# Down projection with 22 of 44 pairs by seven block products, their weight sums made by DRAM-to-DRAM adding transfers

## The chip, the core and the metric

The kernel runs on one core of a Trainium2 chip. The core has a matrix engine (TensorE, PE in the profile, with its weight loads shown apart as PEld), a vector engine (VectorE, DVE), a scalar engine (ScalarE, ACT), a general engine (GpSimd, POOL) and a sync engine that here only issues transfers (SyncE, SP). Each engine works through its own list of instructions in order and waits for the others by semaphores. Sixteen DMA engines move data between the memory off the core (DRAM) and the core's SBUF; they take their work from queues that SP, ACT and POOL feed. The matrix engine adds its products up in a third memory, PSUM.

The metric is the time of one execution on the device in microseconds (us); for several runs the median. The profile comes from one more execution and counts from its first to its last instruction (the span).

## The reference

One encoder block on 256 tokens of 2048 features, in float32. The change touches only the down projection at the end of the gated channel mixer:

```
def conv_glu(hn, w_up, conv_w, conv_b, w_down):
    up = hn @ w_up                                  # 256x2048 @ 2048x11264
    gate, val = jnp.split(up, 2, axis=-1)           # two halves of 5632
    gate = dwconv_centred(gate, conv_w, conv_b)     # three taps along the tokens
    return (jax.nn.gelu(gate, approximate=True) * val) @ w_down   # 256x5632 @ 5632x2048
...
    ff = conv_glu(hn, w_ffn_up[i], ffn_conv_w[i], ffn_conv_b[i], w_ffn_down[i])
    h = h + rmsnorm(ff, ffn_norm_post[i])
```

## The kernel before, in words

**Products in three parts.** float32 values are split into a high part, rounded to the matrix engine's short float32 form, and a low part, the rest. A product of two float32 matrices is then three products: high by high, high by low, low by high. `split` (line 138) does it for weights: a copy on ACT writes the high part (line 147), a subtraction on DVE writes the low part (line 148). Its results rotate through five buffers of 1056 columns for the high and five for the low parts. `raw` (line 151) loads 1 MB of weights over SP's queue into one of three buffers.

**The stages.** In order of time: input projection and the sequence mixers, output projection (`wo`), up projection, down projection (`dn`), gate of the last mixer (`gt`). The up projection runs in 11 slabs of 512 hidden features (loop at line 796). For each slab `feature_pairs` (line 293) is called twice for the gate half (`ga`, weights `ug`) and twice for the value half (`va`, weights `uv`); each call loads two pieces of 1 MB and does 128 products of the matrix engine. So a slab loads eight pieces. Between the two halves comes the convolution on ACT and DVE (line 805), the Gelu on ACT (line 806), and on POOL a multiplication by the tokens' norm factors (line 807). DVE then takes the value sums out of PSUM and multiplies them by POOL's result (line 815) into `hid`, which holds all 5632 hidden features.

**The down projection** (`sublayer("dn", ...)`, line 859) takes the 2048 output columns in two halves. Each half walks over the 5632 hidden features in 22 pairs of 128-feature blocks (`token_major`, line 246); a pair loads 1 MB of `w_down` (two blocks of 128 rows, 1024 columns). A plain pair takes 24 products of 128x512 (two blocks, two token halves, two column halves, three parts).

**Seven block products.** For pairs named in `fast`, `seven_products` (line 201) writes the 2x2 by 2x2 block product with seven products in place of eight, which is Strassen's and Winograd's scheme: 7 times 3 products, 21 in place of 24. It needs sums of weight blocks, which DVE makes in place in the load buffer (lines 209 to 211), and sums of blocks of the hidden values, which `pair_sums` makes (line 709, lines 712 to 715 and the split in lines 716 and 717). It splits 3584 columns of weights (512 + 3 x 1024) where a plain pair splits 2048. Before, pairs 2, 5, 8, 11, 14, 17 of the first half and 2, 5, 8, 11, 14, 17, 19 of the second go this way, 13 in all. `hid_sums` (line 840) keeps the sums of four pairs in two pages for the second half. At the end of each half `combine` (line 222) adds the shared products up in PSUM.

**Buffers.** Pages of 2048 columns rotate through 13 buffers (`page`, line 70). During the up projection the four pages of its input `hf` are among them; they come free at its end. Nothing in the kernel before is issued on POOL's DMA queue.

Of the kernel before, what the change touches and what calls it, by code (L numbers as in the profile page):

```python
# [51 lines left out]
def build(nc, a, out):  # L52
# [5 lines left out]
    with tile.TileContext(nc) as tc, \  # L58
            tc.tile_pool(name="const", bufs=1) as cp, \
            tc.tile_pool(name="weights", bufs=1) as wp, \  # L60
            tc.tile_pool(name="pages", bufs=1) as gp, \
            tc.tile_pool(name="small", bufs=1) as sp, \
            ExitStack() as early, \
            tc.tile_pool(name="pmain", bufs=6, space=bass.MemoryType.PSUM) as pm, \
            tc.tile_pool(name="pmisc", bufs=2, space=bass.MemoryType.PSUM) as pc:

        def ins(r):
            return getattr(r, "ins", r)
# [41 lines left out]
        vt = cp.tile([P, V_N - V_SCW], F32, name="vt")  # L110
        small = ep.tile([P, 80 + 512], F32, name="small")

        last = {}

        def load(dst, src, ahead=False):

            with tc.issue_after(last["dma"]) if last and not ahead else nullcontext():
                return ins(nc.sync.dma_start(dst, src))
# [31 lines left out]

        def raw(name, src, a_, b_):
            r = wp.tile([P, 2048], F32, tag="raw", bufs=3, name=name)
            last["dma"] = load(r[:, :a_ * b_].rearrange("p (a b) -> p a b", a=a_), src, True)
            return r

# [42 lines left out]
                yield o, c  # L198
                c += o.shape[-1]

        def seven_products(name, r, a_, acc, alt, start, stop):

            v = r.rearrange("p (b c) -> p b c", b=4)
            b11 = split(f"{name}a", r[:, :512], 512)
            b2 = split(f"{name}b", r[:, 1024:], 1024)

            nc.vector.tensor_sub(v[:, 0:2], v[:, 1::2], v[:, 0:2])
            nc.vector.tensor_sub(v[:, 3], v[:, 3], v[:, 0])  # L210
            nc.vector.tensor_sub(v[:, 2], v[:, 2], v[:, 3])
            t13 = split(f"{name}c", r[:, :1024], 1024)
            t42 = split(f"{name}d", r[:, 1024:], 1024)
            for x, (wh, wl), c, o, own in (
                    ("a11", b11, 0, alt[0], True), ("a12", b2, 0, acc[0][0], False), ("s4", b2, 512, acc[0][1], False),
                    ("s1", t13, 0, alt[1], True), ("s3", t13, 512, alt[2], True), ("a22", t42, 0, acc[1][0], False),
                    ("s2", t42, 512, alt[3], True)):
                xh, xl = a_[x]
                for q, (xx, ww) in enumerate(((xh, wh), (xh, wl), (xl, wh))):
                    mm(o, xx, ww[:, c:c + 512], own and start and q == 0, own and stop and q == 2)  # L220

        def combine(name, acc, alt, cut):


            m = [mid(f"{name}v{i}") for i in range(2)]
            p1, s16, s165, s167 = (m[i // 2][:, i % 2 * 512:(i % 2 + 1) * 512] for i in range(4))

            def add(o, a_, b):
                nc.vector.tensor_add(o, a_, b)

            nc.scalar.copy(p1, alt[0])
            add(s16, alt[3], p1)
            add(acc[0][0], acc[0][0], p1)
            add(s165, alt[1], s16)
            add(acc[0][1], acc[0][1], s165)
            add(s167, alt[2], s16)
            add(acc[1][0], acc[1][0], s167)
            add(s165, alt[2], s165)
            if cut:
                o = acc[1][1]  # L240
                acc[1][1:] = [o[:, :256], alt[0][:, :256]]
                add(acc[1][2], o[:, 256:], s165[:, 256:])
                s165 = s165[:, :256]
            add(acc[1][1], acc[1][1], s165)

        def token_major(name, w, c0, ks, get, acc, tail=1, fast=(), alt=None, sums=None):


            group, nu = [], len(ks) // 2
            for u in range(nu):  # L250
                k0 = ks[2 * u]
                r = raw(f"{name}r{k0}", w[k0 * P:(k0 + 2) * P, c0:c0 + 1024]
                        .rearrange("(k p) c -> p k c", p=P), 2, 1024)
                if u in fast:
                    if u == fast[0]:
                        alt = alt + [misc(f"{name}s{i}") for i in (2, 3)]
                    seven_products(f"{name}{k0}", r, sums(k0), acc, alt, u == fast[0], u == fast[-1])
                    continue
                for j in range(2):
                    group.append((k0 + j, *split(f"{name}{k0}_{j}", r[:, j * 1024:(j + 1) * 1024], 1024)))  # L260
                if nu - tail <= u < nu - 1:
                    continue

                order = [(t, o, g, q) for t in range(2) for o in columns(acc[t]) for g in group for q in range(3)] \
                    if u == nu - 1 or u - 1 in fast[-1:] else \
                    [(t, o, g, q) for g in group for t in range(2) for q in range(3) for o in columns(acc[t])]
                for t, (o, c), (k, wh, wl), q in order:
                    xh, xl = (v[:, t * P:(t + 1) * P] for v in get(k))
                    xx, ww = ((xh, wh), (xh, wl), (xl, wh))[q]
                    mm(o, xx, ww[:, c:c + o.shape[-1]], k == ks[0] and q == 0, k == ks[-1] and q == 2)  # L270
                if u - 1 in fast[-1:]:
                    combine(name, acc, alt, nu - tail == u + 1 and tail > 1)
                group = []
                aside()
# [434 lines left out]
        def pair_sums(name, s, o, a11, a21, a12, a22):  # L709

            s1, s2, s3, s4 = (s[:, i * P:(i + 1) * P] for i in range(4))
            nc.vector.tensor_add(s1, a21, a22)
            nc.vector.tensor_sub(s3, a11, a21)
            nc.vector.tensor_sub(s2, s1, a11)
            nc.vector.tensor_sub(s4, a12, s2)
            nc.scalar.copy(o[:, :512], s[:, :512])
            nc.vector.tensor_sub(o[:, 512:], s[:, :512], o[:, :512].bitcast(F32))
            return {f"s{i + 1}": (o[:, i * P:(i + 1) * P], o[:, 512 + i * P:512 + (i + 1) * P]) for i in range(4)}
# [70 lines left out]
                      V_FN, Pairs, ((5,), (2, 4)), Sums("cs", cat))  # L789


        pl = [ple(0)]
        rf = row_rstd("rf", h)
        rfb = along_tokens("rfb", rf)
        hid = [page(f"hid{i}") for i in range(6)]
        for s in range(DFF // 512):
            sc = mid(f"gr{s}")
            for i in range(2):
                ga = main(f"ga{s}{i}")
                feature_pairs(f"ug{s}{i}", w_up, s * 512 + i * 256, hf, ga)  # L800
                o = sc[:, i * 512:(i + 1) * 512]
                total(o, ga)
                v = o.rearrange("p (f t) -> p f t", f=2)
                nc.vector.tensor_tensor(v, v, rfb.unsqueeze(1).to_broadcast([P, 2, L]), op=ALU.mult)
            cv = conv(f"fc{s}", sc, 3, V_FCW + 4 * s, NF, V_FCB + 4 * s)
            nc.scalar.activation(cv, cv, AF.Gelu_apprx_tanh)  # L806
            nc.gpsimd.tensor_tensor(cv.rearrange("p (f t) -> p f t", f=4), cv.rearrange("p (f t) -> p f t", f=4),  # L807
                                    rfb.unsqueeze(1).to_broadcast([P, 4, L]), op=ALU.mult)
            for i in range(2):
                va = main(f"va{s}{i}")  # L810
                feature_pairs(f"uv{s}{i}", w_up, DFF + s * 512 + i * 256, hf, va)
                c0 = (s % 2) * 1024 + i * 512
                hd = hid[s // 2][:, c0:c0 + 512]
                total(hd, va)
                nc.vector.tensor_mul(hd, hd, cv[:, i * 512:(i + 1) * 512])
# [19 lines left out]
                hcache[k0], hcache[k0 + 1] = get_hid(k0), get_hid(k0 + 1)  # L835
            return hcache[k]

        keep, kept = [], {}

        def hid_sums(k):  # L840


            (h1, l1), (h2, l2) = get_hid(k), get_hid(k + 1)
            if k not in kept:
                src = hid[k // 8][:, (k % 8) * L:(k % 8 + 2) * L]
                a11, a21, a12, a22 = (src[:, i * P:(i + 1) * P] for i in range(4))
                n = len(kept)
                if n in (0, 2):
                    keep.append(page(f"hsum{k}", F32R))
                o = keep[-1][:, n % 2 * 1024:(n % 2 + 1) * 1024] if n < 4 else mid(f"he{k}", F32R)  # L850
                d = pair_sums(f"hd{k}", mid(f"hd{k}"), o, a11, a21, a12, a22)
                if n < 4:
                    kept[k] = d
            else:
                d = dict(kept[k])
            d.update(a11=(h1[:, :P], l1[:, :P]), a12=(h2[:, :P], l2[:, :P]), a22=(h2[:, P:], l2[:, P:]))
            return d

        hp = sublayer("dn", w_down, list(range(NF)), hid_get, gload("gffn", a["ffn_norm_post"][0]), h, V_PN,
                      fast=((2, 5, 8, 11, 14, 17), (2, 5, 8, 11, 14, 17, 19)), sums=hid_sums)  # L860


        pl.append(ple(1))
# [114 lines left out]
```

## Time and profile before

| | us |
|---|---|
| median of three runs | 1144.42 (1144.21 to 1145.68) |
| the profiled execution | 1143.61 |
| its span | 1141.8 |
| PE busy / DVE busy / ACT busy / POOL busy, of the span | 1122.5 / 871.6 / 609.8 / 123.3 |
| loads of `w_down`: 44 of 1 MB each, median from issue to landing | 5.4 (first half), 5.6 (second) |

The span is what lies between the first and the last instruction; the profiled execution is 1.8 us longer, and the median of the runs 0.8 us above the profiled execution. Two columns of the stage views need a word: the DMA share is the mean busy share of the 16 DMA engines, and GB/s is what they moved in that stretch. Where both are shown, GB/s divided by the share is the rate that this kind of transfer would reach with the engines always busy.

### The profile page before, as it was taken

To read this page: it belongs to the slowest core of one execution; us is meant where nothing else is said; L and a number is where in the kernel's file an instruction comes from. 1 tells how busy PE (TensorE), PEld (TensorE's weight loads), DVE (VectorE), ACT (ScalarE), POOL (GpSimd) and SP (SyncE) were. 2 spreads that over 40 slices of the span, in tenths; PEclk is the share of its full clock that TensorE was granted. 3 is DMA by queue.
4 is the path that set the end of the run, shared out by engine and by line. 5 is a ranking of instruction groups with operands and counts; after the bars stand their busy time and mean duration, and the time that the engine had idled before them with its cause. 6 is when DMAs were issued, how large, how long until landed. Compare 5 with 4: busy or idle time off the path is not lost.

```text
span 1141.8 us, 15452 instructions
## 1 busy us (share of the span) xinstructions
PE 1122.5 (98%) x6018; PEld 967.7 (85%) x6018; DVE 871.6 (76%) x1142; ACT 609.8 (53%) x830; POOL 123.3 (11%) x123
## 2 busy tenths in 40 slices
PE   9998999999999999999999999999999999999996
PEld 9997987888888888888888888888888888887885
DVE  6579796699877666666766666668888898899895
ACT  6633543555674454544544545545555565657562
POOL 0274504200110000000000000000000000002001
PEclk9998999999999999999999999999999999999998
DMA  9952347545556555555555565556466656565652
GB/s 358 340 184 75 111 149 261 201 164 187 168 198 198 195 193 189 184 185 185 185 190 195 181 204 188 185 184 222 154 214 219 199 173 218 178 205 174 210 196 74
DMA packets 129593, 219.04 MB, mean 192 GB/s; under 512 B 3696, under 2 KB 96752, under 8 KB 128624
## 3 DMA queue, kind: packets, MB, share of 16 engines
q1 hardware_dynamic: 129232, 217.70, 57.2%
q8 instruction: 47, 0.77, 0.3%
q10 hardware_dynamic: 288, 0.36, 0.1%
q14 instruction: 26, 0.21, 0.1%
HBM read 215.95 MB, written 2.10 MB: 191 GB/s over the span
## 4 chain that ended last, share of the span: by engine, by line
PE 92%; DVE 5%; ACT 1%; POOL 1%; issue 1%; DMA 0%; DVEq 0%; POOLq 0%; ACTq 0%
PE va L86 22%; PE ga L86 21%; PE dna L86 17%; PE woa L86 7%; PE gt L86 7%; PE dtu L86 4%; PE z L86 4%; PE xbc L86 3%; DVE cv L381 2%; PE dns L86 2%; PE dn1s L86 1%; PE dn0s L86 1%; DVE w L594 1%; DVE xb_0l L148 1%; PE ple L86 1%
## 5 line engine op out<-in xcount | busy, mean ns | idle before, releaser
L86 PE MATMUL ga<-wox,ug_0h 128*128 128x512 f32 x352 | 125.5, 395 | 0.0
L86 PE MATMUL ga<-wox,ug_1h 128*128 128x512 f32 x352 | 125.0, 394 | 0.0
L86 PE MATMUL va<-wox,uv_1h 128*128 128x512 f32 x352 | 124.8, 393 | 0.0
L86 PE MATMUL va<-wox,uv_0h 128*128 128x512 f32 x352 | 124.8, 393 | 0.0
L86 PE MATMUL ga<-wox,ug_1l 128*128 128x256 f32 x352 | 99.1, 282 | 0.0
L86 PE MATMUL ga<-wox,ug_0l 128*128 128x256 f32 x352 | 99.1, 282 | 0.0
L86 PE MATMUL va<-wox,uv_1l 128*128 128x256 f32 x352 | 99.1, 281 | 0.0
L86 PE MATMUL va<-wox,uv_0l 128*128 128x256 f32 x352 | 99.1, 281 | 0.0
L86 PEld LDWEIGHTS va<-wox,uv_1h 128*128 128x128 f32 x352 | 66.1, 188 | 15.0
L86 PEld LDWEIGHTS va<-wox,uv_0h 128*128 128x128 f32 x352 | 66.1, 188 | 15.0
L86 PEld LDWEIGHTS ga<-wox,ug_0h 128*128 128x128 f32 x352 | 66.1, 188 | 14.9
L86 PEld LDWEIGHTS ga<-wox,ug_1h 128*128 128x128 f32 x352 | 66.1, 188 | 14.9
L86 PE MATMUL dna<-dn_0h,hs 128*128 128x512 f32 x248 | 75.8, 393 | 0.0
L86 PE MATMUL dna<-dn_1h,hs 128*128 128x512 f32 x248 | 75.7, 393 | 0.0
L807 POOL TENSOR_TENSOR fc<-fc,rfb 128x1024 f32<-128x1024 f32 x11 | 26.6, 2419 | 440.2 <-ACT fc L806 440.2
L86 PEld LDWEIGHTS ga<-wox,ug_0l 128*128 128x128 f32 x352 | 66.2, 188 | 0.1
L86 PEld LDWEIGHTS ga<-wox,ug_1l 128*128 128x128 f32 x352 | 66.2, 188 | 0.0
L86 PEld LDWEIGHTS va<-wox,uv_0l 128*128 128x128 f32 x352 | 66.2, 188 | 0.0
L86 PEld LDWEIGHTS va<-wox,uv_1l 128*128 128x128 f32 x352 | 66.2, 188 | 0.0
L86 PEld LDWEIGHTS dna<-dn_1h,hs 128*128 128x128 f32 x248 | 46.5, 188 | 10.9
L86 PEld LDWEIGHTS dna<-dn_0h,hs 128*128 128x128 f32 x248 | 46.5, 188 | 10.8
L86 PE MATMUL dna<-dn_0l,hs 128*128 128x512 f32 x124 | 40.2, 393 | 0.0
(1382 smaller groups left out, 2933.6 us busy)
## 6 DMA issues: line engine op xcount, KB each, us to landing
dn0r<-w_ffn_down SPq DMA_DIRECT2D x22, 1024.0 KB, 5.4
dn1r<-w_ffn_down SPq DMA_DIRECT2D x22, 1024.0 KB, 5.6
zr<-w_in SPq DMA_DIRECT2D x8, 1024.0 KB, 5.1
wo0r<-w_out SPq DMA_DIRECT2D x8, 1024.0 KB, 5.4
wo1r<-w_out SPq DMA_DIRECT2D x8, 1024.0 KB, 5.6
gt0r<-w_ple_gate SPq DMA_DIRECT2D x8, 1024.0 KB, 5.5
gt1r<-w_ple_gate SPq DMA_DIRECT2D x8, 1024.0 KB, 6.3
dtur<-w_in SPq DMA_DIRECT2D x14, 528.0 KB, 8.9
```

The lines of the kernel that those rows point to most:

```text
L86: nc.tensor.matmul(o, lhsT, rhs, start=start, stop=stop, skip_group_check=True)
L148: last["dve"] = ins(nc.vector.tensor_sub(lo[:, s], src[:, s], hi[:, s].bitcast(F32)))
L381: nc.vector.scalar_tensor_tensor(o[:, lo:hi], i[:, lo + d:hi + d], vec(wcol + j * wstep + f), o[:, lo:hi], op0=ALU.mult, op1=ALU.add)
L594: nc.vector.scalar_tensor_tensor(w[:, h * P:(h + 1) * P], cbm[:, 0, g, t, :], dt[:, t, 8 * g + h:8 * g + h + 1], w[:, h * P:(h + 1) * P], ...
L807: nc.gpsimd.tensor_tensor(cv.rearrange("p (f t) -> p f t", f=4), cv.rearrange("p (f t) -> p f t", f=4), rfb.unsqueeze(1).to_broadcast([P, ...
```

## The change

22 pairs in place of 13 go by seven products: 2, 4, 6, 8, 9, 11, 13, 14, 16, 18, 19 in the first half and 1, 3, 5, 7, 8, 10, 12, 14, 16, 17, 19 in the second. The sums of their weight blocks are no longer made by DVE in SBUF. For each such pair a DRAM tile of 1 MB is filled by four transfers of POOL's queue: a copy of the two weight blocks (1 MB), an adding transfer of the right columns onto the left (0.5 MB), and two adding transfers of 0.25 MB within the tile. Each waits for the one before it. The signs of the scheme are turned so that every weight sum is an addition. The 22 chains are staggered into 25 jobs, a copy of one pair beside the first addition of the pair before it, and so on; they are put into POOL's list behind the multiplication of each slab of the up projection, three jobs in each of the first three slabs and two in each of the others. Such a pair then loads 0.75 MB of the weights as they are and the 1 MB of sums. The gate projection and `wo` still make their sums on DVE. The sums of hidden values are made anew in each half; nothing is kept.

```
-        def seven_products(name, r, a_, acc, alt, start, stop):
-            v = r.rearrange("p (b c) -> p b c", b=4)
-            b11 = split(f"{name}a", r[:, :512], 512)
-            b2 = split(f"{name}b", r[:, 1024:], 1024)
-            nc.vector.tensor_sub(v[:, 0:2], v[:, 1::2], v[:, 0:2])
-            nc.vector.tensor_sub(v[:, 3], v[:, 3], v[:, 0])
-            nc.vector.tensor_sub(v[:, 2], v[:, 2], v[:, 3])
-            t13 = split(f"{name}c", r[:, :1024], 1024)
-            t42 = split(f"{name}d", r[:, 1024:], 1024)
+        def block_sums(name, w, which):
+            jobs = []
+            def step(c0, k, i):
+                t = sums_[name, c0, k]
+                v = t.rearrange("p (b c) -> p b c", b=4)
+                if i == 0:
+                    nc.gpsimd.dma_start(t.rearrange("p (k c) -> p k c", k=2),
+                                        w[k * P:(k + 2) * P, c0:c0 + 1024].rearrange("(k p) c -> p k c", p=P))
+                elif i == 1:
+                    nc.gpsimd.dma_start(v[:, 0:2], w[k * P:(k + 2) * P, c0 + 512:c0 + 1024]
+                                        .rearrange("(k p) c -> p k c", p=P), accum_op=ALU.add)
+                elif i == 2:
+                    nc.gpsimd.dma_start(v[:, 3], v[:, 0], accum_op=ALU.add)
+                else:
+                    nc.gpsimd.dma_start(v[:, 2], v[:, 3], accum_op=ALU.add)
+            for c0, k in which:
+                sums_[name, c0, k] = dp.tile([P, 2048], F32, tag=f"{name}s{c0}_{k}", bufs=1, name=f"{name}s{c0}_{k}")
+            for j in range(len(which) + 3):
+                jobs.append([lambda a_=(*which[j - i], i): step(*a_) for i in (3, 2, 1, 0) if 0 <= j - i < len(which)])
+            return jobs
+
+        def seven_products(name, stage, w, k0, c0, a_, acc, alt, start, stop):
+            if (stage, c0, k0) in sums_:
+                r = raw(f"{name}r", None, 0, 0)
+                last["dma"] = load(r[:, 512:1536], w[(k0 + 1) * P:(k0 + 2) * P, c0:c0 + 1024], True)
+                last["dma"] = load(r[:, :512], w[k0 * P:(k0 + 1) * P, c0:c0 + 512], True)
+                t = page(f"{name}t")
+                last["dma"] = load(t, sums_[stage, c0, k0], True)
+                b11 = split(f"{name}a", r[:, :512], 512)
+                b2 = split(f"{name}b", r[:, 512:1536], 1024)
...
+            t13 = split(f"{name}c", t[:, :1024], 1024)
+            t42 = split(f"{name}d", t[:, 1024:], 1024)
...
+        dn_fast = (2, 4, 6, 8, 9, 11, 13, 14, 16, 18, 19), (1, 3, 5, 7, 8, 10, 12, 14, 16, 17, 19)
+        ahead = block_sums("dn", w_down, [(c * 1024, 2 * u) for c, f in enumerate(dn_fast) for u in f])
...
-            nc.gpsimd.tensor_tensor(cv.rearrange("p (f t) -> p f t", f=4), cv.rearrange("p (f t) -> p f t", f=4),
-                                    rfb.unsqueeze(1).to_broadcast([P, 4, L]), op=ALU.mult)
+            scaled = nc.gpsimd.tensor_tensor(cv.rearrange("p (f t) -> p f t", f=4), cv.rearrange("p (f t) -> p f t", f=4),
+                                             rfb.unsqueeze(1).to_broadcast([P, 4, L]), op=ALU.mult)
+            with tc.issue_after(ins(scaled)):
+                for job_ in [j for _ in range(-(-len(ahead) // (DFF // 512 - s))) for j in ahead.pop(0)]:
+                    job_()
...
         def hid_sums(k):
             (h1, l1), (h2, l2) = get_hid(k), get_hid(k + 1)
...
+            src = hid[k // 8][:, (k % 8) * L:(k % 8 + 2) * L]
+            d = pair_sums(f"hd{k}", mid(f"hd{k}"), mid(f"he{k}", F32R), *(src[:, i * P:(i + 1) * P] for i in range(4)))
+            return dict(d, a11=(h1[:, :P], l1[:, :P]), a12=(h2[:, :P], l2[:, :P]), a22=(h2[:, P:], l2[:, P:]))
...
         hp = sublayer("dn", w_down, list(range(NF)), hid_get, gload("gffn", a["ffn_norm_post"][0]), h, V_PN,
-                      fast=((2, 5, 8, 11, 14, 17), (2, 5, 8, 11, 14, 17, 19)), sums=hid_sums)
+                      fast=dn_fast, sums=hid_sums)
```

Beside these, `pair_sums` and `combine` change between additions and subtractions of the same size and number, to go with the turned signs.

More of the change, by code (lines that the diff above doesn't have):

```diff
@@ L62, in build @@
             tc.tile_pool(name="small", bufs=1) as sp, \
+            tc.tile_pool(name="dram", bufs=1, space=bass.MemoryType.DRAM) as dp, \
             ExitStack() as early, \
@@ L111, in build @@
         small = ep.tile([P, 80 + 512], F32, name="small")
-        last = {}
+        last, sums_ = {}, {}
         def load(dst, src, ahead=False):
@@ L152, in raw @@
             r = wp.tile([P, 2048], F32, tag="raw", bufs=3, name=name)
+            if src is None:
+                return r
             last["dma"] = load(r[:, :a_ * b_].rearrange("p (a b) -> p a b", a=a_), src, True)
@@ new lines, in seven_products @@
+        def seven_products(name, stage, w, k0, c0, a_, acc, alt, start, stop):
[7 more added lines that the diff above has]
+                b2 = split(f"{name}b", r[:, 512:1536], 1024)
+            else:
+                r = t = raw(f"{name}r", w[k0 * P:(k0 + 2) * P, c0:c0 + 1024]
+                            .rearrange("(k p) c -> p k c", p=P), 2, 1024)
+                b11 = split(f"{name}a", r[:, :512], 512)
+                b2 = split(f"{name}b", r[:, 1024:], 1024)
+                v = r.rearrange("p (b c) -> p b c", b=4)
+                nc.vector.tensor_add(v[:, 0:2], v[:, 0:2], v[:, 1::2])
+                nc.vector.tensor_add(v[:, 3], v[:, 3], v[:, 0])
+                nc.vector.tensor_add(v[:, 2], v[:, 2], v[:, 3])
+            t13 = split(f"{name}c", t[:, :1024], 1024)
+            t42 = split(f"{name}d", t[:, 1024:], 1024)
@@ L226, in combine @@
             p1, s16, s165, s167 = (m[i // 2][:, i % 2 * 512:(i % 2 + 1) * 512] for i in range(4))
-            def add(o, a_, b):
-                nc.vector.tensor_add(o, a_, b)
+            add, sub = nc.vector.tensor_add, nc.vector.tensor_sub
             nc.scalar.copy(p1, alt[0])
-            add(s16, alt[3], p1)
+            sub(s16, p1, alt[3])
             add(acc[0][0], acc[0][0], p1)
             add(s165, alt[1], s16)
-            add(acc[0][1], acc[0][1], s165)
+            sub(acc[0][1], acc[0][1], s165)
             add(s167, alt[2], s16)
@@ L241, in combine @@
                 acc[1][1:] = [o[:, :256], alt[0][:, :256]]
-                add(acc[1][2], o[:, 256:], s165[:, 256:])
+                sub(acc[1][2], o[:, 256:], s165[:, 256:])
                 s165 = s165[:, :256]
-            add(acc[1][1], acc[1][1], s165)
+            sub(acc[1][1], acc[1][1], s165)
         def token_major(name, w, c0, ks, get, acc, tail=1, fast=(), alt=None, sums=None):
@@ L256, in token_major @@
                         alt = alt + [misc(f"{name}s{i}") for i in (2, 3)]
-                    seven_products(f"{name}{k0}", r, sums(k0), acc, alt, u == fast[0], u == fast[-1])
+                    seven_products(f"{name}{k0}", name[:2], w, k0, c0, sums(k0), acc, alt, u == fast[0], u == fast[-1])
                     continue
+                r = raw(f"{name}r{k0}", w[k0 * P:(k0 + 2) * P, c0:c0 + 1024]
+                        .rearrange("(k p) c -> p k c", p=P), 2, 1024)
                 for j in range(2):
@@ L836, in hid_get @@
             return hcache[k]
-        keep, kept = [], {}
         def hid_sums(k):
             (h1, l1), (h2, l2) = get_hid(k), get_hid(k + 1)
[L844 to L857, printed above, removed]
+            src = hid[k // 8][:, (k % 8) * L:(k % 8 + 2) * L]
+            d = pair_sums(f"hd{k}", mid(f"hd{k}"), mid(f"he{k}", F32R), *(src[:, i * P:(i + 1) * P] for i in range(4)))
+            return dict(d, a11=(h1[:, :P], l1[:, :P]), a12=(h2[:, :P], l2[:, :P]), a22=(h2[:, P:], l2[:, P:]))
+        assert not ahead
         hp = sublayer("dn", w_down, list(range(NF)), hid_get, gload("gffn", a["ffn_norm_post"][0]), h, V_PN,
-                      fast=((2, 5, 8, 11, 14, 17), (2, 5, 8, 11, 14, 17, 19)), sums=hid_sums)
+                      fast=dn_fast, sums=hid_sums)
         pl.append(ple(1))
```

6 lines of the change are left out of this document (2 added, 4 removed).

## The prediction

> **What bounds the kernel now.** I read the page's busy shares first, then the chain of waits in order of time, then the two stages that the change touches as stretches, then the loads and POOL's one instruction per slab in the up projection. In the chain (start us, length us, what), at the seam of the two stages:
>
> ```profile
> PE 1122.5 (98%) x6018; PEld 967.7 (85%) x6018; DVE 871.6 (76%) x1142; ACT 609.8 (53%) x830; POOL 123.3 (11%) x123
> ...
> 776.68 22.33 PE va L86 x128
> 799.00 11.11 PE dna L86 x48
> 810.11 0.69 PE dns L86 x3
> ```
>
> Each piece starts where the last one ends: the matrix engine is never left waiting here. A product of 128x512 takes 11.10 / 48 = 0.2313 us of this chain (the 393 ns that the groups give are overlapped). The stretches (us; busy time of PE, PEld, DVE, ACT, POOL with counts; granted clock; DMA share; GB/s):
>
> ```profile
> 330.00:799.00 469.00, 469.00 (x2689) 411.66 (x2688) 315.83 (x402) 236.18 (x314) 26.61 (x11) 1.00 0.58 191
> 799.00:1030.00 231.00, 231.00 (x1002) 187.69 (x1001) 200.91 (x241) 137.23 (x172) 0.91 (x2) 1.00 0.60 196
> ```
>
> PE is full in both. In the down projection DVE is at 87%; the DMA engines are at 58% and 60% while moving 191 and 196 GB/s, so full they would move 191/0.58 = 329 and 196/0.60 = 327. The covers in the up projection are in three places, a load tile's instructions, POOL's in one slab, and DVE's behind it:
>
> ```profile
> L118 SPq DMA_DIRECT2D uv51r<-w_ffn_up x2: 368/368/368, 541.6 to 547.2; - x2
> L147 ACT CAST uv_0h<-uv51r x2: 1048/1049/1050, 553.3 to 558.9; 128x1024 fp32r<-128x1024 f32 x2
> ...
> DMA to landing us min/median/max: 4.9/5.0/5.1
> ...
> 382.54 2.41 POOL L807 TENSOR_TENSOR fc<-fc,rfb 128x1024 f32<-128x1024 f32 x1 [40.98 <-ACT fc L806]
> ...
> 388.50 0.69 DVE L815 TENSOR_TENSOR hid<-hid,fc 128x512 f32<-128x512 f32 x1
> ```
>
> A load is issued 553.3 - 541.6 = 11.7 us before its first use and lands in 5.0: a cover of 6.7 us. POOL's product ends at 384.95 and DVE needs it at 388.50: a cover of 3.55 us.
>
> **The change, part by part, against the profiled execution's 1143.6 us** (the runs' median is 0.8 above it, which I add last).
>
> *Products taken away.* 22 - 13 = 9 more pairs give up 3 products each: 27 x 0.2313 = 6.2 us, all on the path, if the stage stays PE's.
>
> *DVE and ACT in the down projection.* From these groups (busy us, mean ns):
>
> ```profile
> L209 DVE TENSOR_TENSOR dn1r<-dn1r 128x1024 f32<-128x1024 f32 x7 | 8.6, 1222 | 0.1
> L210 DVE TENSOR_TENSOR dn1r<-dn1r 128x512 f32<-128x512 f32 x7 | 4.8, 692 | 0.2
> L717 DVE TENSOR_TENSOR he<-hd,he 128x512 fp32r<-128x512 f32 x5 | 3.4, 686 | 0.8 <-ACT he L716 0.8
> L714 DVE TENSOR_TENSOR hd<-hd,hid 128x128 f32<-128x128 f32 x5 | 1.4, 286 | 0.0
> ```
>
> DVE loses 13 x (1.222 + 0.69 + 0.69) = 33.8 us of weight sums. It gains 9 x (0.684 + 3 x 1.222 - 2 x 1.222) = 17.2 us of splits, and sums of hidden values at 4 x 0.286 + 0.686 = 1.83 us each: 22 fall into this stage where 6 do now (5 of the group above, one into a kept page; the other three are made before 799), 16 x 1.83 = 29.3. Together 200.9 + 12.7 = 214 of the shorter 225 us, 95%. ACT gets 9 x 1.67 + 16 x 0.62 = 25 us more, 162 of 225. Both stay under PE on average, so I cost them at nothing; the cover is the 11 us that DVE has left. Two such pairs in a row (five places) need 2 x (4.35 + 0.685 + 1.83) = 13.7 us of DVE against 9.72 of PE, 4.0 short; today's single pairs with new sums (9.47 against 4.86) are 4.6 short and PE waits for nothing in this stage, so the buffers cover it. Without cover: 5 x 4.0 = 20 us.
>
> *Loads in the down projection.* 22 pairs load 1.75 MB for 1 MB: 17.3 MB more, at 327 GB/s 53 us of full engines. 0.60 x 231 + 53 = 192 of 225 us, 85%. SP's list puts each load of sums where its page comes free, in the order of use, so nothing new waits long there; the first of them waits for a page of the up projection's input at about 799 and is needed after pairs 0 and 1 at about 810. Cost nothing; cover 11 us less the 5.4 that a load takes.
>
> *The transfers on POOL's queue.* This is the open price: no transfer of the trace goes from DRAM to DRAM, none adds, none is issued on this queue. 22 copies of 1.05 MB and as much again of additions (0.5 + 0.25 + 0.25). Spare engine time: a slab of 44.66 us (eight loads of 5.58) holds 8 x 1.05 MB / 329 = 25.5 us of loads, so 19.2 us are free, 211 in 11 slabs. Lower bound: every byte moved once at the best rate of the page's slices, 358 GB/s, 2.9 us per MB, 5.9 us per pair, 129 in all; all hidden, three jobs (17.6) still fit into 19.2. Upper bound: each read and each write costs as much as a load (3.19 us per MB), two for a copy and three for an addition: 16 us per pair, 351 in all, 140 over. I take a copy as a load, since a load too is one read and one write, and an addition as two, since it must read both operands: 3.19 + 6.38 = 9.6 us per pair. Then 22 x 9.6 = 211: the sum just fits, but not its order. The first slab's queue (three copies, 1.25 MB added: 17.5 us) and those of two jobs (19.1) fit; the second and third slabs' three whole jobs take 28.7, 9.5 us over each, and no later slab has room to make it up. What stops PE: POOL issues in order, so the next slab's product stands behind the last of these transfers, whose waits are for landed ones; DVE waits for that product with the next weights' splits behind it. And loads that share the engines land later than their cover of 6.7 us. So 2 x 9.5 = 19.0 us on the path. With sums that cost the engines more than 2 x 3.19 the excess grows by 22 times the difference, with an addition at a copy's price it is gone.
>
> Sum: 1143.6 - 6.2 + 19.0 = 1156.4, as a median 1157.
>
> [...]
>
> **The rivals.**
>
> *All hidden (1138).* The transfers cost between 2.9 and 4.4 us per MB, copies and additions alike, and the loads get their share. For it: 42% of the DMA engines' time is idle in that stage, and a load has 6.7 us of cover. Against it: additions must read twice. 1143.6 - 6.2 + 0.8 = 1138.2, up to 1141 if the second and third slab still slip. It decides where a pair costs under 6.4 us, a third of 19.2.
>
> [...]
>
> [...]
>
> *The down projection gives it back (1144 to 1158).* The stage turns from PE's to DVE's or the loads', at 95% and 85% with double pairs; the products saved are lost in waits of PE at these places, and up to 20 us more. Against it: the covers above.
>
> **Chances.** Forecast 0.38 (1147 to 1180); all hidden 0.37; starved or dearer 0.19 (above 1180, mostly to 1240); given back 0.06, half of it within 0.2% of before. 0.2%, about 2.3 us, is what a measurement of this kernel can tell from no change. So faster 0.37, within 0.2% 0.04, slower 0.59. The range goes from 1137 to 1220, which leaves out little below and a good half of the starved cases above; the forecast's own is 1147 to 1180.
>
> **What would show it.** Right: PE's groups of the down projection lose 27 products and its stretch is near 225 us without PE waits; the up projection lengthens from 11 x 44.66 = 491 us to about 510, its second to fourth slab above all; the DMA share there is at 0.9 or more; POOL's product of the third and fourth slab ends after DVE's need, and DVE waits for POOL. Wrong: a DMA share of 0.8 with PE's pieces still 22.33 us (all hidden); landing times of loads above 11.7 us in every slab and ACT waiting for DMA (starved); PE waiting for DVE between 799 and the end (given back). The number falls with the price of an adding transfer first of all.

## The result, and the profile after

The changed kernel takes 1238.34 us (median of four runs, 1235.25 to 1242.19) against 1144.88 for the kernel before on the same chip: a ratio of 1.082, 95% interval 1.0807 to 1.0833. It is 93 us slower, 81 us above the forecast and outside its range; it lies within 2 us of the 1240 at the far end of "starved or dearer" (chance 0.19).

The page of the changed kernel, its busy shares, the granted clock and the DMA engines by slices, and the two queues (line numbers above 60 have moved; the weights' copy on ACT is L148 now, the subtraction on DVE L149, POOL's product L846):

```profile
PE 1147.7 (93%) x5991; PEld 980.5 (79%) x5991; DVE 867.6 (70%) x1186; ACT 623.9 (50%) x861; POOL 200.6 (16%) x211
...
PEclk9999999999998988989897998989999999999999
DMA  9933375546698989798997989898998668975662
...
q1 hardware_dynamic: 132752, 235.00, 57.6%
q0 software_dynamic: 18304, 46.14, 18.8%
```

PE now stands for 7% of the span, in the middle of it, where the DMA engines went from 58% to 91%. The adding queue (q0) takes 18.8% of the 16 engines' 1237.5 us: 233 us, 10.6 us for each of 22 pairs. The two stages as stretches, parted at 897.39, where the last product of the up projection ends (columns as before: length; busy time of PE, PEld, DVE, ACT, POOL; granted clock; DMA share; GB/s):

```profile
330.00:897.39 567.39, 498.71 (x2686) 429.45 (x2685) 303.61 (x387) 229.06 (x309) 103.66 (x98) 0.92 0.91 235
897.39:1123.40 226.01, 225.20 (x972) 181.66 (x972) 207.69 (x296) 157.37 (x206) 1.40 (x3) 1.00 0.83 287
```

From 330 us on the up projection takes 567.4 us in place of 469; these 98.4 us are more than the 95.7 by which the span grew. For 567.4 - 498.7 = 69 of them PE stands idle; its busy time grows by the other 30 with the same products, at a mean granted clock of 0.92. The down projection is near what the forecast made of it: DVE 207.7 us (214 forecast), ACT 157.4 (162), a DMA share of 0.83 (0.85), and PE idle for 0.8 us.

What ends PE's waits, and then one load tile of the sixth slab, its issue, its first use and its landing:

```profile
PE ga L87 <- ACT ug_0h L148: 52.3, 9, 9.3
PE va L87 <- ACT uv_0h L148: 9.7, 2, 7.6
PE ga L87 <- DVE ug_0l L149: 5.3, 10, 0.8
```

```profile
L119 SPq DMA_DIRECT2D ug51r<-w_ffn_up x2: 367/368/368, 569.6 to 573.7; - x2
L148 ACT CAST ug_0h<-ug51r x2: 1044/1046/1049, 587.2 to 600.5; 128x1024 fp32r<-128x1024 f32 x2
...
  DMA ug51r<-w_ffn_up: 18.3, 2
...
DMA to landing us min/median/max: 17.5/22.1/26.7
```

PE waits for ACT's copy of the weights, and ACT for the load: a load of this tile landed 5.0 us after its issue before and was first used 10.8 us after it; now it takes 17.5 and 26.7 to land. The chain of waits has the same load as one piece, between the last product of a slab and the first of the next:

```profile
573.70 26.66 DMA ug51r<-w_ffn_up
...
601.53 1.24 DVE ug_0l L149
602.77 0.04 issue
602.81 7.33 PE ga L87 x26
```

What runs beside it is POOL's list, put behind the slab's product at 566.07:

```profile
566.07 2.40 POOL L846 TENSOR_TENSOR fc<-fc,rfb 128x1024 f32<-128x1024 f32 x1 [29.54 <-ACT fc L845]
...
570.25 1.76 POOL L213 DMA_DIRECT2D dns<-w_ffn_down  x1
580.04 0.85 POOL L221 DMA_DIRECT2D dns<-dns  x1 [8.03 <-DMA dns<-dns]
585.00 0.81 POOL L219 DMA_DIRECT2D dns<-dns  x1 [4.11 <-DMA dns<-w_ffn_down]
...
618.93 2.39 POOL L846 TENSOR_TENSOR fc<-fc,rfb 128x1024 f32<-128x1024 f32 x1 [28.83 <-ACT fc L845]
```

POOL has issued its last transfer 29 us before the next slab's product, which waits for ACT as it did before. From one such product to the next it is now 50.9 to 57.9 us in the slabs that issue two jobs (mean 53.8), and 58.0 and 61.7 behind the second and third, which issue three, against 44.66. Behind the first, with its three partial jobs, it is 53.4 in place of 43.4.

The records of the trace by queue show who got the engines. Taken over all stretches of 2 us of the up projection in which POOL's queue held more than 0.3 of the engines (310 us of the changed kernel):

```
                    us    loads' share  POOL queue's  loads GB/s  load records per POOL record
changed kernel      310   0.29          0.71           78         1.4
e2_spread           288   0.33          0.72           95         1.5
e3_no_add           244   0.30          0.65           87         1.7
e4_rows1k           300   0.38          0.70          112         1.1
e9_up_only          208   0.30          0.69           95         1.5
mean ns of one record: load 1024 B 53; copy 4096 B 213; addition 2048 B 220 (e4: addition 1024 B 108)
```

The loads need 188 GB/s (8 x 1.05 MB in 44.66 us) and get 78. The other rows belong to the experiments. Shifting the stretches by parts of 2 us moves the loads' share by about 0.01 in the changed kernel and by 0.05 in e9_up_only.

### The profile page after: what moved, and what is told of

The parts are those of the page before. It is cut to its first block, busy times and chain, and to the rows that moved or that the text cites. A ratio compares the mean times of both kernels' runs of the same rounds, so it can differ in the third digit from the quotient of the medians.

```text
span 1237.5 us, 15740 instructions
## 1 busy us (share of the span) xinstructions
PE 1147.7 (93%) x5991; PEld 980.5 (79%) x5991; DVE 867.6 (70%) x1186; ACT 623.9 (50%) x861; POOL 200.6 (16%) x211
## 3 DMA queue, kind: packets, MB, share of 16 engines
q0 software_dynamic: 18304, 46.14, 18.8%
HBM read 279.38 MB, written 48.23 MB: 265 GB/s over the span
## 4 chain that ended last, share of the span: by engine, by line
PE 64%; DMA 24%; DVE 7%; ACT 3%; issue 1%; POOL 1%; DVEq 0%; POOLq 0%; ACTq 0%
PE va L87 14%; PE dna L87 13%; PE gt L87 6%; PE woa L87 6%; PE ga L87 6%; PE z L87 4%; PE dtu L87 3%; PE xbc L87 3%; DMA uv30r<-w_ffn_up 3%; DMA ug61r<-w_ffn_up 3%; DMA uv20r<-w_ffn_up 2%; PE dns L87 2%; DMA ug41r<-w_ffn_up 2%; DMA ug91r<-w_ffn_up 2%; DMA ug11r<-w_ffn_up 2%; DMA ug71r<-w_ffn_up 2%
## 5 line engine op out<-in xcount | busy, mean ns | idle before, releaser
L87 PE MATMUL ga<-wox,ug_0h 128*128 128x512 f32 x352 | 143.4, 438 | 52.3 <-ACT ug_0h L148 52.3
L87 PE MATMUL va<-wox,uv_0h 128*128 128x512 f32 x352 | 128.3, 402 | 9.7 <-ACT uv_0h L148 9.7
L87 PEld LDWEIGHTS ga<-wox,ug_0h 128*128 128x128 f32 x352 | 74.7, 212 | 71.8 <-ACT ug_0h L148 55.2
L87 PE MATMUL ga<-wox,ug_0l 128*128 128x256 f32 x352 | 108.7, 309 | 5.4 <-DVE ug_0l L149 5.3
L87 PEld LDWEIGHTS ga<-wox,ug_0l 128*128 128x128 f32 x352 | 74.6, 212 | 10.7 <-DVE ug_0l L149 10.6
L846 POOL TENSOR_TENSOR fc<-fc,rfb 128x1024 f32<-128x1024 f32 x11 | 26.4, 2401 | 301.3 <-ACT fc L845 301.3
L87 PE MATMUL dna<-dn_0h,hs 128*128 128x512 f32 x176 | 55.1, 395 | 0.7 <-DVE hs L867 0.7
L87 PE MATMUL dna<-dn_1h,hs 128*128 128x512 f32 x176 | 54.6, 393 | 0.0
L87 PEld LDWEIGHTS dna<-dn_0h,hs 128*128 128x128 f32 x176 | 32.7, 188 | 9.2 <-DVE hs L867 1.8
L87 PEld LDWEIGHTS dna<-dn_1h,hs 128*128 128x128 f32 x176 | 33.0, 188 | 7.7
L216 POOL DMA_DIRECT2D dns<-w_ffn_down x22 | 31.3, 1421 | 43.8 <-DMA dns<-w_ffn_down 38.8
```

What stands on the lines that cost most here:

```text
L87: nc.tensor.matmul(o, lhsT, rhs, start=start, stop=stop, skip_group_check=True)
L216: nc.gpsimd.dma_start(v[:, 0:2], w[k * P:(k + 2) * P, c0 + 512:c0 + 1024] .rearrange("(k p) c -> p k c", p=P), accum_op=ALU.add)
L846: scaled = nc.gpsimd.tensor_tensor(cv.rearrange("p (f t) -> p f t", f=4), cv.rearrange("p (f t) -> p f t", f=4), rfb.unsqueeze(1).to_broad ...
```

## The experiments

Two theories stood after the result. *Share*: while POOL's queue runs, the loads get too small a share of the engines, and the cover of 6.7 us runs out in every slab. *Sum*: the engines have more work than time in the up projection, 273 us of loads and 233 of transfers in 469.

**e1_no_sums: no transfers on POOL's queue.** The sums are left out; the weight blocks are loaded in their place, so that the down projection has the same products, splits and loads.

```
-            with tc.issue_after(ins(scaled)):
-                for job_ in [...]: job_()
+            ahead.clear()
...
-                last["dma"] = load(t, sums_[stage, c0, k0], True)
+                last["dma"] = load(t as two blocks, w[k0 * P:(k0 + 2) * P, c0:c0 + 1024], True)
```

> Leaves out the sums of weight blocks: nothing is issued on POOL's DMA queue, and the page of sums is loaded with 1 MB of the weights as they are; loads, products and splits are those of the changed kernel. Theory Share (the loads of the up projection are starved while POOL's queue runs) and theory Sum (the DMA engines have too much to do in all): the up projection is back at the 469 us of the stretch before, the down projection keeps the 27 products saved, 1138 to 1141. Rival (part of the loss lies in the down projection, by DVE at 95% and more loads): 1144 or above, with PE waiting for DVE after the seam.

Measured: 1137.82 us (1136.53 to 1139.52), ratio 0.9943 (0.9927 to 0.996). The stretches of the up projection and of the down projection up to 1025 us:

```profile
330.00:799.00 469.00, 469.00 (x2688) 411.64 (x2688) 312.43 (x390) 234.65 (x311) 26.44 (x11) 1.00 0.58 192
799.00:1025.00 226.00, 226.00 (x981) 183.54 (x980) 208.13 (x295) 158.19 (x206) 0.71 (x3) 1.00 0.82 274
```

No gap in either. So the down projection's part of the change is worth 1144.8 (the kernel before, measured beside it) - 1137.8 = 7.0 us, and the transfers cost 1238.3 - 1137.8 = 100.5.

**e2_spread: the same 88 transfers, not in bursts.** They are let go one to three at a time at 43 points about 11 us apart: behind POOL's product and behind one-column copies on POOL of DVE's results (`pace`).

```
-            with tc.issue_after(ins(scaled)):
-                for job_ in [...]: job_()
+            turn.extend(j for _ in range(...) for j in ahead.pop(0)); pace(scaled)
...
+                mark(hd)       # m = gpsimd.tensor_copy(tiny(...), hd[:, 511:512]); pace(m)
```

> The same transfers on POOL's queue, but a slab's are let go at four points about 11 us apart, each point a one-column copy on POOL that waits for DVE's result of that moment. Share: each run of transfers is now short against the loads' cover, so the loads land in time; what is left is Sum, 278 us of loads and 233 us of POOL's transfers in 491 us, 20 us too much: 1160, between 1148 and 1175. Rival (two queues at once slow each other whatever the order): 1225 to 1240.

Measured: 1168.97 us (1163.96 to 1169.68), ratio 1.0202 (1.018 to 1.0224). Its up projection as one stretch, and the largest wait there:

```profile
330.00:826.70 496.70, 479.00 (x2689) 416.15 (x2688) 304.70 (x388) 227.06 (x310) 133.26 (x128) 0.99 1.00 269
```

```profile
PE ga L87 <- ACT ug_0h L148: 8.6, 5, 3.1
```

Letting go of the same transfers in small groups takes back 69 of the 100 us, although the loads' share in company hardly rises (0.33): what counts is how long they are in company at a stretch. What is left is 31 us, 28 of them in the up projection, at a DMA share of 1.00 over its 497 us: here the engines are full, which is Sum. It falls where the forecast put its excess: from POOL's second and third product, behind which three jobs are let go, to the next it is 55.3 and 54.6 us in place of 44.66, 10.7 and 10.0 too long (9.5 each forecast), and no other interval is more than 5.2 too long.

**e3_no_add: plain copies in place of the additions.** The additions are left out (`accum_op=ALU.add` taken away); bursts and bytes of the transfers stay.

> Leaves out the additions: the three adding transfers of each pair are plain copies of the same rows. By the packets of the changed kernel's profile a pair falls from 10.5 us of all engines (3.4 copy, 7.1 additions) to about 6.5. Share and Sum: bursts of two pairs last some 20 us in place of 28, loads are short by about 1.5 MB against a cover of 1.26, a few us per slab: 1150 to 1180, and the DMA engines no longer full. Rival (the chain of four dependent transfers or their issue on POOL is what costs): 1225 to 1240.

Measured: 1169.89 us (1169.24 to 1170.54), ratio 1.0219 (1.0199 to 1.024). The transfers now take 163 us of the engines in place of 233 (records of 4096 B at 232 ns where the additions had 2048 B at 220), so an added byte costs about twice a copied one. Still in bursts, and with the total well within the 469 us, 32 us are lost; the loads' share in company is 0.30 as before. This is Share almost without Sum: only the second and third slab still have more work than time, by an estimate of 3 x 163 / 22 - 19.2 = 3 us each.

**e4_rows1k: the same additions in rows of 1 KB.** The DRAM tile is padded so that each row of it is 256 elements long and no rows merge; the copy and the first addition are issued as two each. In the trace only the additions have records of 1024 B; the copies keep theirs of 4096 B, 5632 of them as in the changed kernel.

```
-                v = t.rearrange("p (b c) -> p b c", b=4)
+                v = sums_[name, c0, k].rearrange("p (e c) -> p e c", e=8)[:, :, :256]   # tile of 8 * 264
```

> The same sums, but the DRAM tile is padded so that every row of POOL's transfers is 1 KB like a load's (copy and first addition become two transfers each), and the sums' page is loaded in 1 KB rows. If the engines alternate packet by packet between the two queues, a load gets about half of the engine time beside a copy and a third beside an addition, in place of a quarter and a fifth: 1165 to 1205. If each queue gets its share by time, or more packets only cost more: 1235 or above.

Measured: 1189.65 us (1189.57 to 1189.72), ratio 1.0392 (1.0371 to 1.0413). With additions whose records last 108 ns in place of 220, in the same bursts, the loads' share rises from 0.29 to 0.38 (112 GB/s), and 49 us come back; whether the two transfers more per pair had a part in it was not separated. The number of load records for one of POOL's stays between 1.1 and 1.7 in all five kernels of the table, while POOL's records last from 108 to 232 ns: by these counts the loads' part goes with the number of records more than with their length. How the engines divide their time between the two queues, the counts do not tell.

**e5_one_job: ten pairs, one job behind a slab.** Only the first slab issues three, all partial. The other twelve pairs load weight blocks in place of sums (left out).

```
-        ahead = block_sums("dn", w_down, [... for c, f in enumerate(dn_fast) for u in f])
+        ahead = block_sums("dn", w_down, [... for c, f in enumerate(dn_fast) for u in f][::2][:10])
```

> Ten of the 22 pairs get their sums by transfers, one job (four transfers, 10.5 us by the packets of the changed kernel's trace) behind each slab's gelu product; the first slab issues three partial jobs. The other twelve pairs load their weight blocks where the sums would be, so their sums are left out, and the DMA and engine work of the down projection is that of the changed kernel. Theory Share (loads starved while POOL's queue runs): from the changed kernel's stretch 573.7 to 602 us, where two jobs took 28 us, one job takes about 14 us beside the loads, these move at some 75 to 110 GB/s against 188 needed, fall behind by 14 x (1 - 75/188) = 8.4 us at most, and 6.7 us of cover is there: up to 1.7 us of standing in each of the seven full slabs, 1137.8 + 0 to 12 = 1138 to 1150, and the slabs with one job stand far less than half of what slabs with two did (9 us). Theory Sum (engine time alone): 273 + 105 = 378 of 462 us, nothing stands: 1138 to 1140. If a single job costs as much as half of a two-job slab in every slab (loss in proportion to the bytes, 100 / 22 x 10 = 46 us), both fall: 1180 to 1190.

Measured: 1143.06 us (1141.11 to 1147.56), ratio 0.999 (0.998 to 0.9999); 5 us above e1. Ten pairs cost a twentieth of what 22 cost: not in proportion to the bytes, but by what a burst exceeds the cover. In the profiled execution, the slowest of the ten (1147.56), from one of POOL's products to the next it is 49.6 and 46.6 us behind the first two and 44.6 to 44.8 behind all others: single jobs cost nothing, only the first slab's three do. PE's only wait of note in the up projection is 2.6 us for one late `ug_0h`.

**e7_pool_adds: POOL makes the sums itself.** No transfers; in the down projection POOL adds the blocks of the loaded page into another page, three additions per pair.

```
-                nc.gpsimd.dma_start(v[:, 0:2], ..., accum_op=ALU.add)
+                nc.gpsimd.tensor_add(q[:, 0:2], v[:, 0:2], v[:, 1::2])
+                nc.gpsimd.tensor_add(q[:, 3], v[:, 3], q[:, 0])
+                nc.gpsimd.tensor_add(q[:, 2], v[:, 2], q[:, 3])
```

> The 22 pairs' sums are made by POOL's own additions in the down projection (three per pair: 128x1024 and two of 128x512, out of the loaded page into another), with no transfers on POOL's queue and the loads of the kernel before; complete sums. If the theory is right that only the transfers cost time and the down projection's part of the change is a gain of 6 us: the up projection is that of the kernel before, POOL has 22 x (2.42 + 2 x 1.77) = 131 us of work in a stretch of 225 us (durations of its products in the trace of before), DVE 214 us: 1136 to 1141, faster than both kernels. Rival: POOL's additions come late for DVE's splits (load, 6 us of POOL, then 4 us of splits, against three raw buffers of 15 us) or slow DVE's own instructions: the down projection stretches, 1145 to 1165, seen as PE idle on dna<-dn with DVE or POOL behind it.

Measured: 1218.12 us (1217.14 to 1219.49), ratio 1.0649 (1.0633 to 1.0665): the rival, and worse than it said. DVE's groups from 800 to 1030 us, of this kernel and then the same operations in e1_no_sums (busy us, mean ns):

```profile
L865 DVE TENSOR_TENSOR hs<-hid,hs 128x512 fp32r<-128x512 f32 x31 | 35.0, 1128 | 3.5 <-ACT hs L864 3.4
L756 DVE TENSOR_TENSOR he<-hd,he 128x512 fp32r<-128x512 f32 x16 | 18.6, 1163 | 1.4 <-ACT he L755 1.4
L754 DVE TENSOR_TENSOR hd<-hid,hd 128x128 f32<-128x128 f32 x16 | 18.2, 1140 | 0.3
```

```profile
L866 DVE TENSOR_TENSOR hs<-hid,hs 128x512 fp32r<-128x512 f32 x42 | 28.7, 686 | 3.7 <-ACT hs L865 3.6
L755 DVE TENSOR_TENSOR he<-hd,he 128x512 fp32r<-128x512 f32 x21 | 14.4, 687 | 2.1 <-ACT he L754 2.1
L753 DVE TENSOR_TENSOR hd<-hid,hd 128x128 f32<-128x128 f32 x20 | 5.8, 289 | 0.4
```

Beside POOL's additions DVE's own take 1.1 us where they took 0.69 or 0.29; an addition of 128x128 took up to 2.5 us. DVE, not PE, bounds the stage: from 799 to 1095 us it is busy for 286.5 of 296 us, PE for 240.7. The three groups are among those that grew most; the splits in `dn_0l` and `dn_1l` take 1.3 to 1.7 us in place of 1.2. What makes DVE's operations longer, no run shows.

**e6_early: begin in the stages before.** All 22 pairs, complete sums; 28 of the 88 transfers behind POOL's own instructions between 85 and 320 us, the other 60 at 43 points of the up projection.

```
+            if i in (3, 5, 7):
+                early_step(m, {3: 1, 5: 2, 7: 4}[i])       # behind the mixers' products on POOL
...
+            n, now[0] = 60 * (now[0] + 1) // 43 - 60 * now[0] // 43, now[0] + 1
+            early_step(after, n)
```

> All 22 pairs by transfers as in the changed kernel, complete sums, but their 88 transfers are let go one to four at a time from 90 us on: 28 of them behind POOL's own instructions of the mixers, of z and of the output projection (90 to 320 us), the other 60 at 43 points of the up projection, one or two at each, about 11 us apart. Share: no burst is longer than two transfers (5.3 us), within the cover of 6.7 us, so no starving; Sum: in the up projection 273 + 60/88 x 233 = 432 of 462 us, fits with little room. Both expect most of the spread kernel's remaining 31 us to go: 1146 (1138 to 1158). If the loss stays at 20 us or more, then mixing the two queues costs by itself, not the engines' total.

Measured: 1160.61 us (1159.13 to 1164.35), ratio 1.0151 (1.0131 to 1.017): slower than expected, but elsewhere: its first product of the up projection starts at 321.5 us, in e1 at 302.7, and that is 18.8 of the 22.0 us by which its span exceeds e1's. The up projection from 400 to 800 us has no gap, at a DMA share of 0.90 to 0.94; PE's longest new wait is in the mixers:

```profile
PE xt L624 <- DVE cv L635: 6.9, 1, 6.9
```

```profile
DVE w L648 <- POOL w L641: 9.7, 1, 9.7
```

```profile
133.22 0.85 POOL L221 DMA_DIRECT2D dns<-dns  x1 [3.72 <-DMA dns<-dns]
137.49 0.83 POOL L219 DMA_DIRECT2D dns<-dns  x1 [3.42 <-DMA dns<-w_ffn_down]
142.24 1.16 POOL L216 DMA_DIRECT2D dns<-w_ffn_down  x1 [3.92 <-DMA dns<-w_ffn_down]
142.98 2.35 POOL L641 TENSOR_TENSOR w<-cbm,dt 128x1024 f32<-128x1024 f32 x1
```

The last view is POOL's list: three transfers stand one behind the other, each waiting for an earlier one to land, and POOL's product `w`, queued behind them, comes 10 us late for DVE (it started at 132.86 in e2_spread). Loads of the mixers are late too: the chain of waits has one of 11.85 us at 158.66 (`zr`, 5.1 at the shortest), behind which PE waits for 3.9.

**e8_fewer and e9_up_only: a version for use.** Complete sums. e8 lets go of nothing in the mixers: 18 pairs by transfers (60 in the up projection, 12 in four places between 217 and 330 us), 3 with sums on DVE, 21 fast pairs in all. e9 leaves out the places in the output projection too: 16 pairs by transfers (4 at 217 us, 60 in the up projection) and 4 with sums on DVE, 20 fast pairs.

```
+        dn_fast = (2, 4, 6, 8, 11, 13, 14, 16, 18, 19), (1, 3, 5, 7, 10, 12, 14, 16, 17, 19)
+        ahead = block_sums("dn", w_down, [... if (c, u) not in ((0, 4), (0, 16), (1, 10), (1, 16))])
...
+            if t:
+                early_step(e, 4)      # behind the mixers' last norm
```

> Complete sums, 21 of 44 pairs by seven products: 18 of them by transfers (72: 60 at the 43 points of the up projection as in the kernel begun early, where nothing stood there, and 4 each behind POOL's last instruction before two of its longest idle stretches, 33 us after the mixers' last norm and 41 us in the output projection, and 2 + 2 behind the norms before the up projection), 3 with sums on DVE; none is let go in the mixers, where POOL's own product stood behind a waiting transfer. If the loss of the kernel begun early (16 to 22 us) came from there alone: PE loses nothing up to 330 us, the up projection is gapless, DVE in the down projection has 208 + 3 x 2.6 = 216 of 226 us; 1137.8 + 0.7 for the pair less = 1138.5 (1136 to 1142), faster than the kernel before by about 6 us. If the up projection's DMA share of 0.93 costs something by itself or the 60 transfers shift their place and starve a load: 1143 to 1150.

Measured: 1150.92 us (1148.42 to 1151.48), ratio 1.0054 (1.004 to 1.0067): missed. The four transfers let go at 252 us are a burst of their own; in the chain of waits of e8 stands a load of the output projection:

```profile
255.65 13.34 DMA wo10r<-w_out
```

The up projection starts 5.8 us later than in e1, half of the 11.6 us by which e8's span exceeds e1's; the other half, behind that start, was not followed up.

> Complete sums, 20 of 44 pairs by seven products: 16 by transfers (64: 4 behind the mixers' last norm at 217 us, where the last kernel showed no wait, 60 at the 43 points of the up projection, one or two at each), 4 with sums on DVE; none in the output projection, where four together at 252 us made the load wo10r land after 13.3 us and PE stand. If what was left of the loss came from there: PE idle as in the kernel before up to 330 us, the up projection gapless, 1137.8 + 2 x 0.69 for the two pairs fewer = 1139.2 (1137 to 1142), ratio 0.993 to 0.998. If the transfers cost something in the up projection even where nothing stands: 1143 to 1147.

Measured: 1139.78 us (1139.06 to 1140.23), ratio 0.9958 (0.9944 to 0.9971), 1139.2 expected: faster than both kernels, by 4.6 us or 0.4% than the one before. Its up and down projection:

```profile
330.00:799.00 469.00, 469.00 (x2689) 411.61 (x2688) 311.76 (x390) 234.20 (x311) 91.63 (x100) 1.00 0.90 254
799.00:1030.00 231.00, 230.94 (x1001) 187.36 (x1000) 213.10 (x297) 156.46 (x208) 4.75 (x11) 1.00 0.75 257
```

PE is full in both with 60 transfers under the up projection, and the DMA share there is 0.90. The loads' share while POOL's queue runs is 0.30, no better than in the changed kernel, and here it cost nothing. Its 60 transfers go one or two at each of 43 points; two take 5.3 us of the engines (as estimated before e6), so at the queue's 0.69 the loads, at 95 GB/s, fall short by (188 - 95) x 5.3 / 0.69 = 0.7 MB, an estimate, against the 1.3 MB that the cover is worth (6.7 us at 188 GB/s).

## Why the prediction was wrong

- *Products taken away (-6.2).* Right: 7.0 us in e1, 4.6 to 8.4 by its interval.
- *DVE, ACT and loads of the down projection at nothing.* Right: 207.7 us of DVE (6 less than forecast) and 157.4 of ACT in 226, and a DMA share of 0.83, with PE idle for 0.8 us. The double pairs cost nothing that shows, and the rival "given back" fell.
- *Price of the transfers, 9.6 us per pair.* Nearly right: 10.6 by the queue's share; the copy 3.4 (3.19 forecast), the additions 7.1 (6.38). By the forecast's own rule 22 times the difference would have raised the 19.0 to some 40; e2, where the bursts are short and the engines full, lost 31. That an addition costs two copies a byte is what the records have: a 2 KB addition takes 220 ns, a 4 KB copy 213. That a second read is the reason was the author's estimate, and no run shows it: the DRAM reads that the page counts grew by 63.4 MB (215.95 to 279.38), which is the 17.3 of the loads and the 46.1 of POOL's queue taken once.
- *The path, +19.0.* This is the step that failed, in the sentences that two jobs "fit" into a slab and only what is over costs time. They compare totals of a slab, and so assume that the loads lose nothing while their neighbour works. Measured: +100.5, of which 31 are left when the bursts are spread (the total) and 69 are the bursts. The 31 bear out the comparison of totals: in e2 the excess lies in the second and third slab. What it left out is the burst. In a slab with two jobs it runs for some 28 us beside the loads (573.7 to 602); these fall short by (188 - 78) x 28 = 3.1 MB, the cover is worth 1.3 MB, and 1.8 MB at 188 GB/s would be 10 us of standing, an estimate. Measured, such a slab is 9.2 us longer on average (53.84 - 44.66), 6.0 of them PE standing and 3.2 products that ran longer.
- *POOL late, DVE waiting for its product.* This did not occur in the up projection: the product waited for ACT in all 11 slabs. It did occur in e6, in the mixers, where POOL has other work within 10 us.
- *Starved or dearer at 0.19 (above 1180, mostly to 1240).* This is what came, and more by starving than by price: dearer transfers alone would, as said, have made some 40 of the 100.5 us. While POOL's queue runs the loads get 78 of the 188 GB/s that they need; in a slab of two jobs 6.0 us were standing and 3.2 slower products. That loads moved at the same rate in both stages before, with rows of 1 KB and of 4 KB (329 and 327 GB/s), gave no warning: such a rate only says what a byte costs (53 ns for 1 KB, 213 for 4 KB of a copy), not how the engines' time is divided between two queues. No run shows how that is done. With equally many records on both, an estimate from the records' durations is 53 / (53 + 217) = 0.20 for the loads; measured was 0.29, with 1.4 load records for each of POOL's, and 0.38 where the additions' rows were as short as the loads'.
- *Not in the sum at all:* the granted clock. 30 of the 98 us are products that ran longer. In the up projection the records have 85 us at a granted clock of 0.50, and PE is busy for 53 of them; half of that, 27 us, is an estimate of what the lower clock cost.

What stays open: how the engines divide their time between the two queues, and why the loads get 1.1 to 1.7 records for each of POOL's. The split of 31 and 69 us is that of two kernels, since e2 also shifts the places of its transfers. And e6 and e9, whose up projections lose nothing, have both fewer transfers there in all and fewer at each point than e2, so that their total alone makes the difference is likely but not shown.

## What to carry to other kernels

Idle DMA time is not free time (e3 lost 32 us with its total well within the stage): ask for how long at a stretch the new transfers run beside loads that must land (28 us here), multiply by the part of their rate that the loads lose (110 of 188 GB/s), and compare that with the cover of one load (6.7 us, 1.3 MB), before the totals. Let such transfers go one or two at a time, at points further apart than they last (e9: 60 at 43 points about 11 us apart, with PE full), and never ahead of an instruction of the same engine that is soon needed (e6: POOL's product 10 us late). And leave the engines a margin: a share of 0.90 to 0.94 cost nothing here (e9, e6), and 1.00 came with a loss of 31 us (e2).

## What the runs showed of the hardware

In the changed kernel's up projection PE stands ten times for more than 2 us, 2.1 to 9.3 us each. With each of these stops goes a stretch in which the granted clock is 0.50; it begins 2.3 to 5.0 us after the stop does, outlasts it by 4.1 to 7.3 us, and the clock is 1.00 behind it. For one of them, PE had stood for 5.00 us before a first product at 601.55 and resumed at 602.81; two stretches from there on (the granted clock is the third column from the right):

```profile
601.55:608.38 6.83, 6.36 (x19) 5.08 (x20) 6.02 (x8) 4.49 (x8) 0.00 (x0) 0.50 0.91 294
608.38:615.20 6.82, 6.82 (x40) 5.98 (x40) 6.75 (x12) 4.94 (x8) 0.00 (x0) 1.00 0.73 236
```

The first stretch has 19 products in 6.36 us of busy time, the second 40 in 6.82: half the clock for 6.83 us cost some 3 us behind this stop, an estimate from these two lines, on top of the stop itself. In the whole trace the granted clock is either 0.50 or 1.00, and the stretches of 0.50 in the up projection, eleven with one behind two shorter stops (1.45 and 0.76 us), last 3.4, 6.8, 10.2 or 13.7 us, 85 us in all. The second surprise is e7's: beside additions on POOL, DVE's additions and subtractions took 1.6 to 4 times as long on average in the three groups shown (1.13, 1.16 and 1.14 us against 0.69, 0.69 and 0.29).
